# Loading the first group of gates in six parts, ordering one cast behind the U tiles, and multiplying the last V tiles half by half

## The chip, the cores and the metric

The kernel runs on one core of a Trainium2 chip. TensorE (PE in the rows) multiplies, VectorE (DVE) and ScalarE (ACT) do the elementwise work, GpSimd (POOL) issues the indirect gathers, and SyncE (SP) issues every other transfer. PEld is TensorE's weight load. The metric is device time in microseconds (us), the median of several executions; the profile is one further execution with the hardware profiler on. About 0.5% of the time (8 us) is what a measurement of this kernel can tell from no change.

## What is computed

The reference is one layer of a streaming encoder for 544 tokens (512 of a prompt, 32 of a running stream) and 1024 channels. It projects, convolves, attends and normalises, and then applies a "PEER" block, in which this change lies. For each token, 8 heads pick 16 out of 16384 experts each. With `e` the picked rows and `g` the softmax of their scores:

```
a = jnp.einsum('td,thkd->thk', tb, u_tab[e])
a = jax.nn.gelu(a, approximate=False) * g
return jnp.einsum('thk,thkd->td', a, v_tab[e])
```

Then `x = layer_norm(alpha * x + g2 * out)` is stored. `u_tab` and `v_tab` have 16384 rows of 1024 floats, 64 MB each.

## The kernel before, in words

The first 384 tokens (NA, three row tiles, TA = 3) are done densely: every expert is computed for every token, and a gate that is zero where an expert was not picked does the choosing. The other 160 tokens are done by gathers: POOL fetches one expert row per token at a time (`gather`, L893), and DVE multiplies it. The gathers are paced by the dense tiles: each waits for a matmul that an earlier dense tile recorded (ANCHOR).

**Dense work.** The experts are split into 128 tiles j of 128 experts. `u_part(j)` (L953) loads 512 KB of `u_tab`, ACT casts it to a high part `hi` and DVE subtracts to get the low part `lo` (`split`, L943 to L951; three raw buffers, two of hi and lo). PE does 24 matmuls of 384 columns into one of two PSUM tiles `pat` (L959), and ACT evacuates it by Gelu (L965). While 26 tiles have room in SBUF, later results go through one of two buffers `gs` and are stored to `ge_d` in DRAM (L967).

`v_part(j)` (L1012) multiplies that Gelu by the gates (P, DVE, L1025), casts P to Ph (ACT, L1028), subtracts to get Pl (DVE, L1030), and splits 512 KB of `v_tab`. `v_mm` (L1035) then does 18 matmuls of 512 columns for a whole tile: three row tiles i, two halves hf of 512 channels, three products (L1042), each accumulating in one of six PSUM banks `accs[i][hf]` over all j.

**Gates.** `onehots(i)` (L835) makes the gates of 16 tokens at a time: four one-hot tiles on DVE, 32 small matmuls (L874), evacuations into `stg` (L875), and one 1 MB store to `g_d` in DRAM (L876). There are 24 such blocks (NBLK), eight for each row tile i. The gates come back for eight tiles j at a time into a tile `gc` of two buffers (L1013 to L1016): 24 blocks x 128 partitions with 512 bytes each, 1536 KB. The pool of `gc` is opened after the pools of the one-hots are closed (L1002), so that it lies in memory which these used.

**Order.** U tiles run while the one-hots are made, a planner (`slot`, L980) doling out background work between them. When the last gates are made, 8 more U tiles follow (EXTRA, L997); then the V tiles begin, and the U tiles that remain are interleaved with them (L1067 to L1072). The last four V tiles are prepared together (L1084) and multiplied with the row tile i as the outer loop, so that the three row tiles end one after the other. `tail` and `norm_tile` (L1046) then do, for each row tile: a product with g2 for each half (L1050), the sum with x (L1052), the squares on ACT (L1055), and the rest on DVE (L1056 to L1062), then two stores (L1063).

The program is written tile by tile, and a scheduler orders each engine's instructions by a simulated timeline before the program runs. On the chip each engine, and SP's queue of transfers, keeps that order: an instruction that waits holds up all that stand behind it on its engine. A manual dependency of the kind ORD (no semaphore, order alone) can be given to the scheduler. Transfers of SP share one hardware queue (q1), those of POOL another (q0), on the same 16 DMA engines.

Of the kernel before, what the change touches and what calls it, by code (L numbers as in the profile page):

```python
# [13 lines left out]
AF = mybir.ActivationFunctionType  # L14
# [12 lines left out]
NA = 384  # L27
# [14 lines left out]
NBLK = NA // GB  # L42
JC = 8
# [32 lines left out]
def build(tc, I, O):  # L76
# [3 lines left out]
    V, S, G, PE, SY = nc.vector, nc.scalar, nc.gpsimd, nc.tensor, nc.sync  # L80
# [5 lines left out]
    g_d = dram.tile([NBLK, 128, NK, GB], F32, name="g_d")  # L86
# [6 lines left out]
    def pat():  # L93
        return pa.tile([128, 512], F32, tag="pa", name="pat")
# [4 lines left out]
    def sm():  # L99
        return ps.tile([128, 512], F32, tag="sm", name="sm")  # L100
# [136 lines left out]
    U = cp.tile([128, 4, UW], F32, name="U")  # L237
# [28 lines left out]
    ORD = mybir.DependencyInfo(mybir.DependencyClass.NoSync, mybir.DependencyReason.DATA)  # L266
# [45 lines left out]
    for n in range(2):  # L312
        wv = [wsplit(I["w_v"][n, kh]) for kh in range(2)]
        wf = WRAW[-2:]
        for i in range(NT):
            p = pat()
# [7 lines left out]
            else:  # L324
# [6 lines left out]
                p = sm()  # L331
# [249 lines left out]
    for s in range(2):  # L581
        t = op_.tile([128, D], F32, tag="row", name="bg", bufs=4) if s == 0 else xhB[0]
# [356 lines left out]
    h2B = xhB  # L939

    GE = {}

    def split(src, pl=None, nr=RAWB, nh=HIB):  # L943
        pl = pl or uvp
        raw = pl.tile([128, D], F32, tag="raw", name="raw", bufs=nr)
        SY.dma_start(raw, src)
        hi = pl.tile([128, D], F32R, tag="hi", name="hi", bufs=nh)
        S.copy(hi, raw)  # L948
        lo = pl.tile([128, D], F32R, tag="lo", name="lo", bufs=nh)
        V.tensor_sub(lo, raw, hi.bitcast(F32))  # L950
        return hi, lo  # L951

    def u_part(j):  # L953
        hi, lo = split(I["uT"][j])
        p = pat()
        n = 0
        for a, b in ((hi, h2h), (lo, h2h), (hi, h2l)):
            for k in range(KC):
                mm = PE.matmul(p[:, :NA], a[:, k * 128:(k + 1) * 128], b[:, k, :], start=(n == 0), stop=(n == 23))  # L959
                if n == 0:  # L960
                    ANCHOR.append(mm)
                n += 1
        full = sum(g is not None for g in GE.values()) >= ND - 1
        ge = dn.tile([128, NA], F32, tag="gs" if full else "ge", name="ge", bufs=2 if full else ND)
        S.activation(ge, p[:, :NA], AF.Gelu)  # L965
        if full:
            SY.dma_start(ge_d[j], ge)  # L967
            GE[j] = None
        else:
            GE[j] = ge  # L970

# [20 lines left out]
    ahead = 0  # L992
    while state["A"] < TA:
        u_part(ahead)
        ahead += 1
        slot(COST_U, BURST_G)
    for _ in range(EXTRA):  # L997
        u_part(ahead)
        ahead += 1
        slot(COST_U, BURST_G)  # L1000
# [9 lines left out]
    GC = {}  # L1010

    def v_part(j):  # L1012
        if j % JC == 0:  # L1013
            GC[0] = gcp.tile([128, NBLK, JC, GB], F32, tag="gc", name="gc")
            SY.dma_start(GC[0].rearrange("p b j t -> p b (j t)"),
                         g_d[:, :, j:j + JC, :].rearrange("b i j t -> i b (j t)"))  # L1016
        ge = GE.pop(j)
        if ge is None:
            ge = gcp.tile([128, NA], F32, tag="gel", name="gel", bufs=3)
            SY.dma_start(ge, ge_d[j])  # L1020
        early = NK - LAST <= j < NK - 2
        pp, tags = (dn, ("ge",) * 3) if early else (vpp, ("P", "Ph", "Pl"))
        nb = ND if early else 2
        P = pp.tile([128, NA], F32, tag=tags[0], name="P", bufs=nb).rearrange("p (b t) -> p b t", t=GB)
        V.tensor_mul(P, ge.rearrange("p (b t) -> p b t", t=GB), GC[0][:, :, j % JC, :])  # L1025
        Ph = pp.tile([128, NA], F32R, tag=tags[1], name="Ph", bufs=nb)
        Pf = P.rearrange("p b t -> p (b t)")
        S.copy(Ph, Pf)  # L1028
        Pl = pp.tile([128, NA], F32R, tag=tags[2], name="Pl", bufs=nb)
        V.tensor_sub(Pl, Pf, Ph.bitcast(F32))  # L1030
        vp_ = (uvp, RAWB, HIB) if early else (vpp, VRAWB, VHIB)
        vh, vl = split(I["vd"][j * 128:(j + 1) * 128, :], *vp_)
        return Ph, Pl, vh, vl

    def v_mm(j, tiles, parts):  # L1035
        Ph, Pl, vh, vl = parts
        for i in tiles:
            sl = slice(i * 128, (i + 1) * 128)
            for hf in range(2):
                hs = slice(hf * 512, (hf + 1) * 512)  # L1040
                for n, (a, b) in enumerate(((Ph, vh), (Pl, vh), (Ph, vl))):
                    mm = PE.matmul(accs[i][hf], a[:, sl], b[:, hs], start=(j == 0 and n == 0), stop=(j == NK - 1 and n == 2))  # L1042
                    if i == hf == n == 0:
                        ANCHOR.append(mm)
# [21 lines left out]
    for j in range(NK - LAST):  # L1066
        v_mm(j, range(TA), v_part(j))  # L1067
        slot(COST_V)
        while ahead < NK and ahead < j + 3 + lead * (NK - j) // NK:
            u_part(ahead)  # L1070
            ahead += 1
            slot(COST_U)  # L1072
        if ahead == NK and not full:
            full = True
            hx.close()
            fp = pool(ctx, "fp", 1)
            l2g, l2b, g2p, x3, g2s, f3 = [fp.tile([128, D], F32, name=n) for n in ("l2g", "l2b", "g2p", "x3", "g2s", "f3")]
            assert state["gdone"] >= 256
            for dst, src in ((g2p, mod_d[0, 5 * D:6 * D]), (l2g, I["ln2_g"]), (l2b, I["ln2_b"]), (g2s, mod_d[1, 5 * D:6 * D])):
                SY.dma_start(dst, bcast_rows(src, 128))  # L1080
            SY.dma_start(x3, x1_d[TA * 128:TA * 128 + 128])
            norm_tile(3, x3, f3, [accB[0][:, :512], accB[0][:, 512:]], g2p)
    run(gat)
    vs = {j: v_part(j) for j in range(NK - LAST, NK)}  # L1084
    for i in range(TA):
        for j in vs:
            v_mm(j, (i,), vs[j])

    def late(ld):
        tc.add_manual_dep(ld.ins, ANCHOR[-12].ins.name, DEP, reason="paced by the dense tiles")  # L1090
# [13 lines left out]
    for q in range(2):  # L1104
        p = pat()
# [85 lines left out]
```

## Time and profile before

| | us |
|---|---|
| median of 3 runs | 1627.64 (1625.81 to 1632.98) |
| the profiled execution's own time | 1643.86 |
| its span, first to last instruction | 1642.1 |

The profiled execution is 16.2 us (1.0%) longer than the median of the runs. Its span leaves 1.8 us of its own time outside. The rows are of that one execution: they show where time goes and how long each step takes, and a difference worked out from them is taken off the median of the runs.

### The profile page before, as it was taken

The numbers are of one execution on the slowest core, as the hardware profiler recorded it, in microseconds if no ns is written. First come the engines' busy times: TensorE is split into PE (matmuls) and PEld (weight loads), VectorE is DVE, ScalarE is ACT, GpSimd is POOL, SyncE is SP. The second block draws the span as 40 slices with busy tenths as digits, with TensorE's granted clock in tenths as the row PEclk, the third lists the DMA queues.
The fourth block names the chain that finished last, engine by engine and source line by source line (L and its number), as shares of the span: only waits on it lengthen the run. The fifth ranks groups of instructions, "written<-read, shape, count | busy, mean of one in ns | idle before, by whom it ended". The sixth has DMA issues, their size and how long they took to land.

```text
span 1642.1 us, 24695 instructions
## 1 busy us (share of the span) xinstructions
PE 1558.6 (95%) x8887; PEld 1341.7 (82%) x8887; DVE 1387.8 (85%) x2680; ACT 612.7 (37%) x1059; POOL 503.6 (31%) x325
## 2 busy tenths in 40 slices
PE   7999987999989998999899899999999999999996
PEld 4777854786669997999899789888888888888885
DVE  3788888899999997999798568888878787788898
ACT  3312456333122443444445333333333333333342
POOL 0000000000145356259534124544333333344440
PEclk9999987999999999999999999999999999999998
DMA  9767333274478887999999999999999999999993
GB/s 345 281 196 252 89 116 117 87 234 133 153 254 278 289 283 270 329 355 333 332 344 365 372 325 306 344 342 374 332 351 350 338 339 343 341 328 330 347 336 106
DMA packets 184537, 465.58 MB, mean 284 GB/s; under 512 B 17536, under 2 KB 85184, under 8 KB 181216
## 3 DMA queue, kind: packets, MB, share of 16 engines
q1 hardware_dynamic: 138336, 296.23, 52.5%
q0 software_dynamic: 46080, 167.79, 28.9%
q8 instruction: 69, 1.13, 0.3%
q14 instruction: 52, 0.43, 0.1%
HBM read 415.57 MB, written 45.77 MB: 281 GB/s over the span
## 4 chain that ended last, share of the span: by engine, by line
PE 67%; DVE 16%; DMA 7%; issue 6%; ACT 2%; SPq 1%; POOL 0%; DVEq 0%; ACTq 0%; POOLq 0%
PE acc L1042 31%; PE pat L959 22%; PE big L194 3%; PE pat L733 2%; PE big L874 2%; DVE jkg L906 2%; DVE lo L950 2%; DMA rowg<-in_u_ji_dram,idx 1%; PE pat L154 1%; PE big L622 1%; DVE s L712 1%; DVE acc L275 1%; DVE accB L917 1%; DVE IT L714 1%; DMA raw<-in_vd_dram 1%
## 5 line engine op out<-in xcount | busy, mean ns | idle before, releaser
L895 POOL DMA_INDIRECT rowg<-in_u_ji_dram,idx x160 | 205.1, 1282 | 794.1 <-DVE VT L709 441.4
L950 DVE TENSOR_TENSOR lo<-raw,hi 128x1024 fp32r<-128x1024 f32 x256 | 312.9, 1225 | 104.8 <-ACT hi L948 97.8
L895 POOL DMA_INDIRECT rowg<-in_vd_dram,idx x160 | 296.7, 1855 | 297.5 <-DVE accB L917 65.7
L948 ACT CAST hi<-raw 128x1024 fp32r<-128x1024 f32 x256 | 266.8, 1047 | 293.7 <-PE acc L1042 196.8
L1042 PE MATMUL acc<-hi,Pl 128*128 128x512 f32 x768 | 298.1, 391 | 0.0
L1042 PE MATMUL acc<-lo,Ph 128*128 128x512 f32 x768 | 276.3, 389 | 0.0
L1042 PE MATMUL acc<-hi,Ph 128*128 128x512 f32 x768 | 245.6, 391 | 6.6 <-issue 5.2
L959 PE MATMUL pat<-h2h,lo 128*128 128x384 f32 x1024 | 210.6, 343 | 18.7 <-DVE lo L950 18.7
L959 PE MATMUL pat<-h2h,hi 128*128 128x384 f32 x1024 | 210.0, 340 | 4.4 <-ACT ge L965 2.7
L906 DVE SCALAR_TENSOR_TENSOR jkg<-rowg,xhB 128x1024 f16<-128x1024 f32 x160 | 195.3, 1220 | 17.9 <-DMA rowg<-in_u_ji_dram,idx 15.7
L959 PE MATMUL pat<-h2l,hi 128*128 128x384 f32 x1024 | 209.1, 341 | 0.0
L917 DVE SCALAR_TENSOR_TENSOR accB<-rowg,wB,accB 128x1024 f32<-128x1024 f32 x158 | 203.0, 1285 | 6.2 <-DMA rowg<-in_vd_dram,idx 5.7
L959 PEld LDWEIGHTS pat<-h2h,lo 128*128 128x128 f32 x1024 | 182.4, 191 | 22.9 <-DVE lo L950 19.8
L959 PEld LDWEIGHTS pat<-h2h,hi 128*128 128x128 f32 x1024 | 179.3, 188 | 11.6 <-ACT ge L965 3.5
L959 PEld LDWEIGHTS pat<-h2l,hi 128*128 128x128 f32 x1024 | 183.6, 191 | 2.6
L1042 PEld LDWEIGHTS acc<-hi,Ph 128*128 128x128 f32 x768 | 144.3, 189 | 33.1 <-issue 5.5
L1042 PEld LDWEIGHTS acc<-hi,Pl 128*128 128x128 f32 x768 | 145.0, 189 | 27.6 <-issue 0.5
L1042 PEld LDWEIGHTS acc<-lo,Ph 128*128 128x128 f32 x768 | 144.1, 188 | 28.0
L965 ACT ACTIVATE ge<-pat 128x384 f32<-128x384 f32 x128 | 62.7, 491 | 208.9 <-PE pat L959 136.3
L1028 ACT CAST Ph<-P 128x384 fp32r<-128x384 f32 x128 | 65.0, 510 | 145.7 <-issue 81.8
L275 DVE SCALAR_TENSOR_TENSOR acc<-U,wdw,acc 128x574 f32<-128x574 f32 x120 | 96.7, 806 | 1.5
L1030 DVE TENSOR_TENSOR Pl<-P,Ph 128x384 fp32r<-128x384 f32 x128 | 70.8, 554 | 28.3 <-ACT Ph L1028 27.3
(322 smaller groups left out, 1880.3 us busy)
## 6 DMA issues: line engine op xcount, KB each, us to landing
raw<-in_uT_dram SPq DMA_DIRECT2D x128, 512.0 KB
raw<-in_vd_dram SPq DMA_DIRECT2D x128, 512.0 KB
wr<-in_w_ada_dram SPq DMA_DIRECT2D x48, 512.0 KB
g_d<-stg SPq DMA_DIRECT2D x24, 1024.0 KB
gc<-g_d SPq DMA_DIRECT2D x16, 1536.0 KB
wq<-in_w_query_dram SPq DMA_DIRECT2D x32, 512.0 KB
ge_d<-ge SPq DMA_DIRECT2D x70, 192.0 KB
gel<-ge_d SPq DMA_DIRECT2D x70, 192.0 KB
```

The source lines that it names most:

```text
L194: PE.matmul(p[h], a[:, k * 128:(k + 1) * 128], b[:, k, h * HT:(h + 1) * HT], start=(q == 0 and k == 0), stop=(q == 2 and k == KC - 1))
L275: t = V.scalar_tensor_tensor(acc[:, c], U[:, c, w:w + CO], wdw[:, c, w:w + 1], acc[:, c], op0=OP.mult, op1=OP.add)
L895: g = G.indirect_dma_start(out=t, out_offset=None, in_=tab, in_offset=bass.IndirectOffsetOnAxis(ap=idx, axis=0))
L906: V.scalar_tensor_tensor(jk, t, 1.0, h2B[s], op0=OP.mult, op1=OP.mult, accum_out=aB[s][:, q:q + 1])
L917: V.scalar_tensor_tensor(ac, t, w[:, q - c0:q - c0 + 1], ac, op0=OP.mult, op1=OP.add)
L948: S.copy(hi, raw)
L950: V.tensor_sub(lo, raw, hi.bitcast(F32))
L959: mm = PE.matmul(p[:, :NA], a[:, k * 128:(k + 1) * 128], b[:, k, :], start=(n == 0), stop=(n == 23))
L965: S.activation(ge, p[:, :NA], AF.Gelu)
L1028: S.copy(Ph, Pf)
L1030: V.tensor_sub(Pl, Pf, Ph.bitcast(F32))
L1042: mm = PE.matmul(accs[i][hf], a[:, sl], b[:, hs], start=(j == 0 and n == 0), stop=(j == NK - 1 and n == 2))
```

## The change

There are three edits. The first group of gates (j = 0) is loaded by six transfers, of the blocks 0 to 7, 8 to 15, 16 to 19, 20 and 21, 22, and 23, where it was one transfer of all 24; the other 15 groups stay as they are. The cast of the first P to Ph is ordered behind the Gelu of the last U tile issued before the V tiles, which is the eighth extra one. And the last four V tiles are multiplied with the half hf outside the tile j: for each row tile, twelve matmuls of the first half and then twelve of the second, where the halves had alternated with every tile.

```
-        S.activation(ge, p[:, :NA], AF.Gelu)
+        LASTU[0] = S.activation(ge, p[:, :NA], AF.Gelu)
...
-            SY.dma_start(GC[0].rearrange("p b j t -> p b (j t)"),
-                         g_d[:, :, j:j + JC, :].rearrange("b i j t -> i b (j t)"))
+            parts = (0, 8, 16, 20, 22, 23, 24) if j == 0 else (0, NBLK)
+            for b0, b1 in zip(parts, parts[1:]):
+                SY.dma_start(GC[0][:, b0:b1].rearrange("p b j t -> p b (j t)"),
+                             g_d[b0:b1, :, j:j + JC, :].rearrange("b i j t -> i b (j t)"))
...
-        S.copy(Ph, Pf)
+        t = S.copy(Ph, Pf)
+        if j == 0:
+            tc.add_manual_dep(t.ins, LASTU[0].ins.name, ORD, reason="behind the U tiles ahead of V")
...
-    def v_mm(j, tiles, parts):
+    def v_mm(j, tiles, parts, halves=(0, 1)):
...
-            for hf in range(2):
+            for hf in halves:
...
     for i in range(TA):
-        for j in vs:
-            v_mm(j, (i,), vs[j])
+        for hf in range(2):
+            for j in vs:
+                v_mm(j, (i,), vs[j], (hf,))
```

## Rows read from the trace of the kernel before

**Rows 1.** The page's head: span, and each engine's busy time, share and instructions.

```profile
span 1642.1 us, 24695 instructions
PE 1558.6 (95%) x8887; PEld 1341.7 (82%) x8887; DVE 1387.8 (85%) x2680; ACT 612.7 (37%) x1059; POOL 503.6 (31%) x325
```

**Rows 2.** Busy time by stretch around the start of V, then TensorE's granted clock, DMA share, GB/s.

```profile
900.00:930.00 30.00, 25.71 (x151) 25.07 (x148) 16.85 (x15) 9.42 (x13) 8.31 (x8) 1.00 1.06 390
930.00:950.00 20.00, 16.32 (x63) 13.23 (x64) 12.68 (x20) 6.98 (x11) 2.38 (x2) 0.83 1.04 338
950.00:1000.00 50.00, 50.00 (x265) 46.91 (x264) 33.04 (x46) 19.33 (x26) 14.74 (x13) 1.00 0.93 318
```

**Rows 3.** The chain of waits, 880 to 950: start us, us, what.

```profile
907.42 10.81 DMA ge_d<-ge
...
918.80 8.61 PE pat L959 x48
```

**Rows 4.** Timeline of PE: start, us, instruction, count, idle before and what ended it.

```profile
899.75 0.64 PE L874 MATMUL big<-Yg,X 128*128 128x128 f16 x8
...
918.80 1.67 PE L959 MATMUL pat<-h2h,hi 128*128 128x384 f32 x8 [1.70 <-ACT ge L965]
...
932.64 0.76 PE L1042 MATMUL acc<-hi,Ph 128*128 128x512 f32 x1 [5.23 <-issue]
933.20 0.63 PE L1042 MATMUL acc<-hi,Pl 128*128 128x512 f32 x1
...
937.47 0.43 PE L1042 MATMUL acc<-hi,Pl 128*128 128x512 f32 x1
...
948.49 1.66 PE L959 MATMUL pat<-h2h,hi 128*128 128x384 f32 x8 [1.04 <-ACT ge L965]
```

**Rows 5.** Timeline of ACT and DVE around the first P.

```profile
929.01 1.03 DVE L1025 TENSOR_TENSOR P<-ge,gc 128x384 f32<-128x384 f32 x2 [3.42 <-DMA gc<-g_d]
...
929.65 0.94 ACT L1028 CAST Ph<-P 128x384 fp32r<-128x384 f32 x2 [5.32 <-DVE P L1025]
...
931.50 1.04 ACT L948 CAST hi<-raw 128x1024 fp32r<-128x1024 f32 x1 [0.91 <-DMA raw<-in_vd_dram]
...
932.81 1.04 ACT L948 CAST hi<-raw 128x1024 fp32r<-128x1024 f32 x1 [0.27 <-DMA raw<-in_vd_dram]
```

**Rows 6.** Timeline of SP's queue: start of issue, time to issue, transfer.

```profile
901.04 0.32 SPq L876 DMA_DIRECT2D g_d<-stg  x1
...
907.42 3.18 SPq L967 DMA_DIRECT2D ge_d<-ge  x2
...
911.64 0.45 SPq L1015 DMA_DIRECT2D gc<-g_d  x1
912.14 11.37 SPq L946 DMA_DIRECT2D raw<-in_vd_dram  x3
923.55 0.85 SPq L1015 DMA_DIRECT2D gc<-g_d  x1
924.45 12.24 SPq L1020 DMA_DIRECT2D gel<-ge_d  x3
...
937.27 0.38 SPq L967 DMA_DIRECT2D ge_d<-ge  x1
```

**Rows 7.** The page's transfer issues: the gate groups, their number and size.

```profile
gc<-g_d SPq DMA_DIRECT2D x16, 1536.0 KB
```

**Rows 8.** Timeline of PE at its end.

```profile
1629.05 0.39 PE L1042 MATMUL acc<-hi,Pl 128*128 128x512 f32 x1
1629.28 0.39 PE L1042 MATMUL acc<-lo,Ph 128*128 128x512 f32 x1
```

**Rows 9.** Timeline of DVE in the tail.

```profile
1620.64 1.29 DVE L1050 TENSOR_TENSOR ff<-acc,g2p 128x512 f32<-128x512 f32 x2 [0.93 <-PE acc L1042]
...
1623.58 1.37 DVE L1050 TENSOR_TENSOR ff<-acc,g2p 128x512 f32<-128x512 f32 x2 [0.20 <-PE acc L1042]
...
1637.41 1.42 DVE L1062 SCALAR_TENSOR_TENSOR x<-x,st,l2b 128x512 f32<-128x512 f32 x2
```

More of the change, by code (lines that the diff above doesn't have):

```diff
@@ L941, in build @@
     GE = {}
+    LASTU = [None]
     def split(src, pl=None, nr=RAWB, nh=HIB):
```

## The prediction, made before the changed kernel was run

> **What bounds the kernel now.** I read the page's head first: PE is busy for 1558.6 of 1642.1 us [rows 1], so only its idle time and its slow stretches can be won. The views by stretch came next. From 950 to 1000 us PE is busy for 50.00 of 50.00 us, with U and V tiles mixed; around the start of V it is not: 25.71 of 30.00 us from 900 to 930, and 16.32 of 20.00 from 930 to 950, there with a granted clock of 0.83. The DMA share beside it is 1.06 and 1.04 [rows 2]: the transfers are as full as PE is meant to be.
>
> The timeline of PE gives the places [rows 4]. PE idles 1.70 us before the U tile at 918.80, 5.23 us before the first V matmul at 932.64, and 1.04 us before 948.49. After the long idle the matmuls run slowly: from 933.20 to 937.47 there are ten steps of 0.427 us, where steps at the full clock take 0.23 us (1629.05 to 1629.28) [rows 4, 8]. That is the lower of the clock's two levels, 1.2 against 2.4 GHz. Ten steps of 0.20 us and a first one of 0.56 for 0.23 lost 2.33 us.
>
> The chain of waits and the other timelines say why. The U tile at 918.80 waited for a Gelu, which waited for a store of an earlier result (issued 907.42, 10.81 us on its way) to free one of two buffers [rows 3, 4]. V waited for the gates: the group was issued at 911.64, and the first P had it at 929.01, 17.4 us later; Ph followed at 929.65 [rows 5, 6]. The `v_tab` load issued right behind, at 912.14, let its cast start at 931.50 [rows 5, 6]. So SP's transfers come one after the other through a full queue: what stands ahead delays what stands behind.
>
> The tail is the other place. DVE idles 0.93 and 0.20 us before the products of the first two row tiles and has little idle after that; PE's last matmul starts at 1629.28 and DVE's last pair at 1637.41 [rows 8, 9].
>
> **The change, part by part.** The durations are of the profiled execution (1643.86 us, of which 1642.1 are its span); the runs' median is 16.2 us less, and I take the sum off that median.
>
> *Six parts.* All but the last part need only gates stored before 901.04, the last store [rows 6]. Their memory was the one-hots', which the last one-hot matmul at 899.75 frees [rows 4]. So 23 of 24 blocks can enter the queue some 10 us earlier, and the last, 64 KB, stands where the whole load stood, with the same wait for the last store; behind that wait on SP are the three `v_tab` loads, the second group and the loads of spilled results, as before [rows 6]. Five more issues cost SP at most 0.85 us each, the longest issue of a group [rows 6], 4.25 us; they are hidden by the queue itself, which held SP for 11.37 and 12.24 us at the next issues. Without that cover they would delay the stores of U results by as much.
>
> What is gained: V no longer waits for the gates. With all of the two later holes gone, 5.23 + 2.33 + 1.04 = 8.60 us.
>
> What is paid: the early parts stand ahead of `u_tab` loads and of the store issued at 907.42. A group is 1536 KB, 1.573 MB [rows 7]; 23/24 of it at the stretch's 390 GB/s [rows 2] takes 3.86 us. The price is between 0 (they fill gaps in the queue) and 23/24 of the store's 10.81 us, 10.4 us. I take 3.86, as the share of 1.06 leaves no gaps. The 1.70 us hole becomes 5.56 us. A hole of 5.23 us brought the slow clock and one of 1.70 did not [rows 4]; 5.56 is nearer to the former, so 2.33 us more are paid (between 0 and 2.33).
>
> The Trainium skill has a rule against this edit (DMA: Bandwidth & Descriptors, Bandwidth): batch transfers to at least 1 MiB, since 64 KB reach only 138 GB/s. It also gives about 2.0 us of fixed time for each transfer (Anatomy of one DMA), so that by an estimate from that page five more would take 10 us if nothing overlapped. The two queued `v_tab` loads of this case disagree, 1.31 us apart.
>
> In rows: those casts, at 931.50 and 932.81 [rows 5], both waited for their loads, and 524 KB in 1.31 us is 400 GB/s, about the stretch's mean. A queued transfer below 1 MB pays nothing visible here. I take 0; the other end is a rival below.
>
> *The order of the cast.* Ph(0) now stands behind the eighth extra Gelu on ACT. From 900.2 to 927.4 PE does six U tiles in 27.2 us (two took 8.61 [rows 3]): two that the loop began, and four of the eight. Four more, 4 x 4.17 = 16.7 us, move ahead of V. The edit adds no instruction. What is queued behind the cast waits with it: on ACT the next Ph and the casts of `v_tab`, on DVE Pl(0), on PE all V tiles. POOL's gathers are paced by whichever dense tiles run, so they go on through the U tiles. Moved U tiles cost nothing as long as their loads, and the stores of their results, keep pace. The step from the last Gelu to Ph and V costs between 0 and 1.04 us (the idle before 948.49, where PE also waited for a Gelu [rows 4]); I take 0, since the mixed stretch after 950 has no idle [rows 2] and a later U tile can fill it.
>
> *Half by half.* The 72 matmuls, their weight loads and operands stay. The first half of each row tile is complete 12 matmuls earlier, 2.7 us, so DVE can do its product while PE does the second. DVE is then nearly full to its end, so what can go is its waiting, 0.93 + 0.20 = 1.13 us [rows 9]; below, 0, or a loss of that size if the fourth tile's operands, now wanted at the tenth matmul instead of the nineteenth, come late. I take 0.93, the longer wait. SP's final stores move with DVE.
>
> *Sum.* -8.60 + 3.86 + 2.33 - 0.93 = -3.34 us, so 1627.64 - 3.34 = 1624.3 us. A measurement here can tell about 0.5%, 8.1 us, from no change: the forecast is **no measurable difference**.
>
> **The rivals.**
>
> *A: the holes simply close.* The early parts cost nothing, and the clock never falls: -8.60 - 0.93 = -9.5 us, 1618.1; with the 1.70 us hole and all of the tail's waits gone, -11.4 and 1616.2. For it: four more U tiles give PE 16.7 us of work just where it had none. Against: the DMA share of 1.06.
>
> *B: V is held back behind starved U tiles, slower.* The fifth extra U tile needs a PSUM buffer, hence the Gelu of the third, hence room in `gs`, hence the store of the first. That store was issued at 937.27, behind the second gate group (923.55) and three loads that held SP for 12.24 us [rows 6]. If that order stays, PE finishes the fourth tile at 927.4 + 3.9 = 931.3 and then has nothing, as V may not start. It goes on between 941 (an early landing, 3.7 us after the issue) and 948.5, where it went on before [rows 4]; four tiles later, at 957.7 to 965.2, V starts after 1.0 us of casts. Before, the same work was behind PE at 932.64 + 16.7 + 2.33 + 1.04 = 952.7. So V comes 6.0 to 13.5 us late; less the tail's 0.93, 1632.7 to 1640.2. It decides where that store stands in SP's order: ahead of the second group, no loss. For it: SP's order before. Against: the scheduler works out a new order.
>
> *C: the parts come no earlier.* SP's order may leave them at 911.64, or their memory may come free late. Then the split does nothing, the order alone moves U tiles into the holes or gives as much back, and the time is 1627.64 - 0.93 = 1626.7.
>
> *D: each part occupies the queue for a fixed time.* With 1.31 us for each of five more, as for a 512 KB load, 6.6 us join the delay: 1624.3 + 6.6 = 1630.9. The page's fixed time of about 2.0 us is of this kind; its rule is named above.
>
> **How the numbers follow.** Forecast 0.35, A 0.28, B 0.20, C 0.12, D 0.05. A is faster by over 0.5% (below 1619.5); B is counted as slower, though its near end is not over 0.5% (above 1635.8); the rest is within. So faster 0.28, same 0.52, slower 0.20. The range reaches down past A's end of 1616.2 by the runs' own scatter (1.8 us), to 1614, and up to the middle of B, 1637, and leaves out the upper half of B and what no case holds. The likeliest case's own range: with its price at 0, 1620.4; at 10.4 us, 1630.8.
>
> **What would show it.** The split is right if five parts are issued between 900 and 905 and the first P no longer waits for a gate group. The price is right if PE's idle before the third extra U tile grows from 1.70 us to about 5.6. The order is right if eight U tiles follow the last one-hot's two before any V matmul, and the 5.23 us hole with its slow steps is gone. B is right if PE idles for about 10 us or more before the fifth of these tiles, with a store of `ge_d` as the cause. The half order is right if DVE's first product of each row tile starts before PE has ended that tile. I am wrong if the idle between 900 and 970 falls below 2 us, or if stretches after 970, where PE is full, get holes that no edit touches.

## The result, and the profile after

The changed kernel is **slower**: 1643.15 us median of 6 runs (1637.81 to 1644.88), against 1633.43 of the kernel before in 6 runs beside it; ratio 1.0067, interval 1.0046 to 1.0087. That is 7.5 to 14.2 us. The forecast was 1624.3, no measurable difference; the time lies above the range's upper end of 1637. Of the 18.9 us between the two, 5.8 are the base: the forecast was taken off a median of 1627.64 from three runs, and before's median beside the change is 1633.43. Rival B, V held back behind starved U tiles, had 0.20.

The two profiled executions can't be set against each other as wholes: 1643.86 us for before, 1642.47 for after. The order of each engine's instructions is the same in both programs up to SP's first load of gates, yet before's execution reached the last one-hot matmul at 899.75 [rows 4] and after's at 880.95. Before's had lost time in two holes that after's does not have (e2's and e4's below have one such each); why only some executions have them is not shown. Timeline of PE, before:

```profile
650.59 2.93 PE L959 MATMUL pat<-h2h,lo 128*128 128x384 f32 x8 [6.80 <-DVE lo L950]
...
802.77 2.93 PE L959 MATMUL pat<-h2h,lo 128*128 128x384 f32 x8 [5.73 <-DVE lo L950]
```

So I compare from the last one-hot matmul on. The head of the page and the busy time by stretch of the changed kernel (after the engines: granted clock, DMA share, GB/s) answer to [rows 1, 2]:

```profile
span 1639.7 us, 24733 instructions
...
PE 1552.5 (95%) x8887; PEld 1335.9 (81%) x8887; DVE 1386.2 (85%) x2680; ACT 611.5 (37%) x1059; POOL 474.3 (29%) x325
```

```profile
900.00:930.00 30.00, 13.12 (x65) 12.80 (x66) 12.52 (x16) 5.32 (x7) 4.27 (x5) 0.72 1.09 366
930.00:950.00 20.00, 18.01 (x103) 17.37 (x101) 11.04 (x16) 6.65 (x10) 4.28 (x4) 1.00 0.76 246
950.00:1000.00 50.00, 50.00 (x243) 43.91 (x242) 38.29 (x50) 16.18 (x23) 17.98 (x16) 1.00 0.89 302
```

PE is busy for 13.12 of 30.00 us where before it was for 25.71 [rows 2], while the DMA share is still above 1. From 950 to 1000 both are full. The timeline of PE shows one long hole, in answer to [rows 4]:

```profile
880.95 0.63 PE L874 MATMUL big<-Yg,X 128*128 128x128 f16 x8
...
899.83 1.66 PE L960 MATMUL pat<-h2h,hi 128*128 128x384 f32 x8 [1.52 <-ACT ge L966]
...
925.31 2.93 PE L960 MATMUL pat<-h2h,hi 128*128 128x384 f32 x8 [16.88 <-ACT ge L966]
928.03 2.08 PE L960 MATMUL pat<-h2h,lo 128*128 128x384 f32 x8
929.95 1.55 PE L960 MATMUL pat<-h2l,hi 128*128 128x384 f32 x8
931.33 1.55 PE L960 MATMUL pat<-h2h,hi 128*128 128x384 f32 x8
...
937.18 1.66 PE L960 MATMUL pat<-h2h,hi 128*128 128x384 f32 x8 [1.53 <-ACT ge L966]
...
946.24 1.67 PE L960 MATMUL pat<-h2h,hi 128*128 128x384 f32 x8 [0.46 <-ACT ge L966]
```

The tile at 925.31 is the fifth extra U tile. Idle times sum to 1.52 + 16.88 + 1.53 + 0.46 = 20.39 us. After the long one, two groups of eight matmuls take 2.72 and 1.92 us, step to step, where the next eight take 1.38: 1.88 us more. The granted clock of the first of these stretches is 0.50, the lower level, and 1.00 in the last (views by stretch):

```profile
925.31:928.03 2.72, 2.72 (x8) 2.72 (x9) 2.65 (x5) 0.49 (x1) 1.16 (x1) 0.50 1.04 416
929.95:931.33 1.38, 1.38 (x9) 1.38 (x9) 0.00 (x0) 0.00 (x0) 0.00 (x0) 1.00 1.05 406
```

With the idle times that is 22.27 us. The same sum for before is 1.70 + 5.23 + 1.04 + 2.33 = 10.30 [rows 4, 8]. The difference, 11.97 us, lies within the measured 7.5 to 14.2. It is not all that sets these two executions apart: from the last one-hot matmul to the end they take 742.3 and 758.8 us. The changed kernel's has two more holes, at 1005.14 (0.63 us) and here, with some 2 us of slow steps behind it:

```profile
1048.00 1.16 PE L1047 MATMUL acc<-hi,Ph 128*128 128x512 f32 x3 [1.80 <-ACT Ph L1031]
```

Before's has one of 1.41 us at 1590.83. These later holes are not the slowdown's cause: e1 below has the same loss without the two. SP's queue and ACT say where it comes from; SP's rows answer to [rows 6]:

```profile
892.79 10.66 SPq L1018 DMA_DIRECT2D gc<-g_d  x6
903.49 1.52 SPq L947 DMA_DIRECT2D raw<-in_vd_dram  x3
907.06 0.38 SPq L1018 DMA_DIRECT2D gc<-g_d  x1
908.73 8.02 SPq L1023 DMA_DIRECT2D gel<-ge_d  x2
916.84 0.38 SPq L947 DMA_DIRECT2D raw<-in_uT_dram  x1
917.26 0.43 SPq L1023 DMA_DIRECT2D gel<-ge_d  x1
917.79 0.38 SPq L968 DMA_DIRECT2D ge_d<-ge  x1
```

```profile
922.66 1.04 ACT L949 CAST hi<-raw 128x1024 fp32r<-128x1024 f32 x1 [8.18 <-DMA raw<-in_uT_dram]
924.76 0.49 ACT L966 ACTIVATE ge<-pat 128x384 f32<-128x384 f32 x1 [1.06 <-DMA ge_d<-ge]
```

The Gelu that frees PE's PSUM buffer runs at 924.76. It waited for the store issued at 917.79, and ahead of it on ACT stood a cast that waited 8.18 us for weights issued at 916.84. Both issues stand behind all that V loads first: gates, `v_tab` tiles, the second group, stored Gelus. Before the change PE did V in this stretch and did not wait for that queue, with no idle time from 932.64 to 947.45; now V may not start.

### The profile page after: what moved, and what is told of

Read it like the earlier page. It is cut to its first block, busy times and chain, and to the rows that moved or that the text cites. A ratio compares the mean times of both kernels' runs of the same rounds, so it can differ in the third digit from the quotient of the medians.

```text
span 1639.7 us, 24733 instructions
## 1 busy us (share of the span) xinstructions
PE 1552.5 (95%) x8887; PEld 1335.9 (81%) x8887; DVE 1386.2 (85%) x2680; ACT 611.5 (37%) x1059; POOL 474.3 (29%) x325
## 4 chain that ended last, share of the span: by engine, by line
PE 66%; DVE 13%; DMA 10%; issue 5%; ACT 3%; SPq 1%; POOL 1%; DVEq 0%; ACTq 0%; POOLq 0%
PE acc L1047 27%; PE pat L960 23%; PE big L194 3%; PE pat L733 2%; PE big L874 2%; DMA raw<-in_vd_dram 2%; DMA rowg<-in_u_ji_dram,idx 2%; PE pat L194 2%; DVE jkg L906 1%; DVE lo L951 1%; DMA raw<-in_uT_dram 1%; PE pat L154 1%; DVE s L712 1%; PE big L622 1%; DVE accB L917 1%
## 5 line engine op out<-in xcount | busy, mean ns | idle before, releaser
L895 POOL DMA_INDIRECT rowg<-in_u_ji_dram,idx x160 | 214.4, 1340 | 777.8 <-DVE VT L709 436.2
L895 POOL DMA_INDIRECT rowg<-in_vd_dram,idx x160 | 258.1, 1613 | 323.1 <-PE acc L1047 97.4
L1047 PE MATMUL acc<-lo,Ph 128*128 128x512 f32 x768 | 290.9, 390 | 0.0
L1047 PE MATMUL acc<-hi,Ph 128*128 128x512 f32 x768 | 238.8, 390 | 1.8 <-ACT Ph L1031 1.8
L917 DVE SCALAR_TENSOR_TENSOR accB<-rowg,wB,accB 128x1024 f32<-128x1024 f32 x158 | 202.1, 1279 | 17.9 <-DMA rowg<-in_vd_dram,idx 17.5
L960 PE MATMUL pat<-h2l,hi 128*128 128x384 f32 x1024 | 204.6, 339 | 0.0
L1035 DVE TENSOR_TENSOR Pl<-P,Ph 128x384 fp32r<-128x384 f32 x128 | 70.6, 552 | 19.4 <-ACT Ph L1031 17.4
```

Of the source, the lines that this page charges most:

```text
L895: g = G.indirect_dma_start(out=t, out_offset=None, in_=tab, in_offset=bass.IndirectOffsetOnAxis(ap=idx, axis=0))
L917: V.scalar_tensor_tensor(ac, t, w[:, q - c0:q - c0 + 1], ac, op0=OP.mult, op1=OP.add)
```

## The experiments

Each kernel was timed in 5 rounds beside the kernel before on the same chip. "Hole" is the longest idle time of PE between the last one-hot matmul and the mixed stretch, "sum" all of its idle times over 0.3 us there, "end" the time from the start of PE's last row in its timeline (the last V matmul; in e6 and e7 the four matmuls of the sample tile) to the end of the span, all of the one profiled execution. Holes behind that stretch, 0 to 6.7 us in all, are in none of these columns.

| kernel | hole | sum | end | median | ratio (interval) |
|---|---|---|---|---|---|
| before | 5.23 | 7.97 | 12.8 | - | 1 |
| changed | 16.88 | 20.39 | 13.2 | 1643.15 | 1.0067 (1.0046 to 1.0087) |
| e1 order alone | 17.69 | 21.78 | 12.9 | 1643.13 | 1.0064 (1.0043 to 1.0086) |
| e2 parts alone | 5.30 | 7.85 | 13.0 | 1636.00 | 1.0023 (1.0000 to 1.0045) |
| e3 halves alone | 5.45 | 8.00 | 12.8 | 1636.21 | 1.0024 (0.9997 to 1.0052) |
| e4 changed, V's later loads behind the stores | 10.27 | 13.37 | 13.2 | 1635.84 | 1.0014 (0.9992 to 1.0036) |
| e5 changed, four `gs` | 14.06 | 15.57 | 13.2 | 1638.15 | 1.0053 (1.0029 to 1.0077) |
| e6 before, four `gs` | 1.67 | 3.18 | 24.2 | 1633.93 | 1.0025 (1.0003 to 1.0047) |
| e7 before, V's later loads behind the stores | 5.65 | 7.17 | 24.2 | 1642.57 | 1.0075 (1.0049 to 1.0102) |
| e8 order alone, four `gs` | 14.65 | 16.16 | 12.9 | 1635.32 | 1.0028 (1.0009 to 1.0046) |
| e9 as e6, sample rows ahead | 1.51 | 2.03 | 17.3 | 1633.05 | 0.9976 (0.9951 to 1.0001) |
| e10 order alone, V's loads from GpSimd | 10.63 | 17.39 | 12.9 | 1642.49 | 1.0032 (1.0005 to 1.0058) |
| e11 as e8, U's weights ahead | 3.73 | 5.24 | 17.5 | 1631.03 | 0.9988 (0.9968 to 1.0009) |
| e12 as e9, sample rows further ahead | 1.65 | 3.16 | 14.6 | 1624.53 | 0.9945 (0.9923 to 0.9968) |

The medians belong to different chips: before's were 1632.88 beside e1 to e4, 1631.63 beside e5 to e8, 1638.87 beside e9 and e10, and 1632.19 beside e11 and e12. The ratios are what compares.

### Which of the three parts costs

e1 keeps the changed kernel's order of the cast and undoes the rest; e2 and e3 keep the parts and the halves alone. On the changed kernel, e1 and e3 undo the parts:

```diff
-            parts = (0, 8, 16, 20, 22, 23, 24) if j == 0 else (0, NBLK)
+            parts = (0, NBLK)
```

e2 and e3 undo the order of the cast:

```diff
-        if j == 0:
-            tc.add_manual_dep(t.ins, LASTU[0].ins.name, ORD, reason="behind the U tiles ahead of V")
```

e1 and e2 undo the halves:

```diff
-        for hf in range(2):
-            for j in vs:
-                v_mm(j, (i,), vs[j], (hf,))
+        for j in vs:
+            v_mm(j, (i,), vs[j])
```

> Theory (the order): with V held behind the last Gelu, PE has nothing between the fourth and the fifth extra U tile, because the fifth needs a PSUM buffer that a Gelu frees only when the first extra tile's store has landed, and that store stands behind the second gate group on SP. The idle before the fifth extra tile is 10 to 17 us, as in the changed kernel (16.88 us), and the time is 8 to 12 us above the kernel before (ratio 1.005 to 1.007). Rival (the parts): six transfers in place of one hold up SP's queue, so that the order alone, with one load, is within 2 us of the kernel before and has no idle over 6 us there.

> Theory (the order): the parts stand where the one load stood in SP's order, so that V starts at about the same place: idle of 4 to 7 us before the first V matmul, as before (5.23 us), and a time within 2 us of the kernel before. Rival (the parts): the six parts take some 10 us to issue, the first P or the stores come late by as much, and the time is 8 to 12 us above (ratio 1.005 to 1.007).

> Both theories: the stretch around the start of V is as before. For the tail: if the waits of DVE for a row tile's second half were on the path, 0.9 us are won; if the tail is a full row of DVE work, the time from PE's last matmul to the end stays at 12.8 to 13.2 us and the time is within 1 us of the kernel before. I expect the latter.

The order alone gives a loss as large, 1.0064 against 1.0067, and the same hole (17.69 us, 0.7 over the range I gave), in the timelines of PE and of SP:

```profile
928.61 2.93 PE L960 MATMUL pat<-h2h,hi 128*128 128x384 f32 x8 [17.69 <-ACT ge L966]
```

```profile
894.95 0.38 SPq L1018 DMA_DIRECT2D gc<-g_d  x1
895.38 11.34 SPq L947 DMA_DIRECT2D raw<-in_vd_dram  x3
906.77 0.43 SPq L1018 DMA_DIRECT2D gc<-g_d  x1
907.24 12.66 SPq L1023 DMA_DIRECT2D gel<-ge_d  x3
...
920.48 0.38 SPq L968 DMA_DIRECT2D ge_d<-ge  x1
```

The parts win nothing. V's first matmul still waits 5.30 us in e2 and 5.45 in e3, which loads the gates whole. From the first gate load's issue to the first P it is 17.68 us with six parts in e2 (915.24 - 897.56; timelines of SP and of DVE):

```profile
897.56 11.01 SPq L1018 DMA_DIRECT2D gc<-g_d  x6
```

```profile
915.24 1.03 DVE L1028 TENSOR_TENSOR P<-ge,gc 128x384 f32<-128x384 f32 x2 [3.86 <-DMA gc<-g_d]
```

and 17.4 with one load [rows 5, 6]. Nor do they hold up what stands behind them: from that issue to the first extra tile's store is 25.00 us with six parts (917.79 - 892.79 in the changed kernel) and 25.53 with one in e1 (920.48 - 894.95). The time that SP stood at `v_tab`, 11.34 us, it now stands at the parts, 10.66.

The halves win nothing either: the end stays 12.8 us long. DVE's timeline in e3 shows waits of 0.94 and 0.41 us at the products, where before had 0.93 and 0.20 [rows 9]:

```profile
1606.73 1.89 DVE L1053 TENSOR_TENSOR ff<-acc,g2p 128x512 f32<-128x512 f32 x3 [0.94 <-PE acc L1045]
...
1610.36 0.69 DVE L1053 TENSOR_TENSOR ff<-acc,g2p 128x512 f32<-128x512 f32 x1 [0.41 <-PE acc L1045]
```

Both ratios are a little over 1, 3 to 4 us, where I had expected to be within 2 and 1 us; with intervals that reach 1.0000 and below, neither can be told from no change.

### Is it the store, and its place in SP's queue

e4 orders the second gate group and the first six loads of stored Gelus behind the last extra tile's store; e7 does that to the kernel before. In e4:

```diff
-            SY.dma_start(ge_d[j], ge)
+            LASTST[0] = SY.dma_start(ge_d[j], ge)
...
+    AHEAD = [LASTST[0].ins.name]
...
-                SY.dma_start(GC[0][:, b0:b1].rearrange("p b j t -> p b (j t)"),
-                             g_d[b0:b1, :, j:j + JC, :].rearrange("b i j t -> i b (j t)"))
+                ld = SY.dma_start(GC[0][:, b0:b1].rearrange("p b j t -> p b (j t)"),
+                                  g_d[b0:b1, :, j:j + JC, :].rearrange("b i j t -> i b (j t)"))
+                if j == JC:
+                    tc.add_manual_dep(ld.ins, AHEAD[0], ORD, reason="behind the stores of the U tiles ahead")
...
-            SY.dma_start(ge, ge_d[j])
+            ld = SY.dma_start(ge, ge_d[j])
+            if j < ND + 6:
+                tc.add_manual_dep(ld.ins, AHEAD[0], ORD, reason="behind the stores of the U tiles ahead")
```

e5 (changed kernel), e6 (before) and e8 (order alone) give `gs` four buffers instead of two, so that a Gelu waits for a store two tiles further back:

```diff
-        ge = dn.tile([128, NA], F32, tag="gs" if full else "ge", name="ge", bufs=2 if full else ND)
+        ge = dn.tile([128, NA], F32, tag="gs" if full else "ge", name="ge", bufs=4 if full else ND)
```

> The changed kernel with the second gate group and the first six loads of spilled results ordered on SP behind the store of the last U tile ahead of V. Theory (the order, through the stores): the idle of 16.88 us before the fifth extra U tile falls below 4 us, V starts after all eight with no wait for its gates, and the time is 4 to 8 us below the kernel before (ratio 0.995 to 0.998), 14 to 18 us below the changed one. Rival (the parts, or the full queue itself): the stores still land late, the idle only moves to another U tile, and the time stays 6 us or more above the kernel before.

> The kernel before (one load, no order of the cast, halves alternating) with the second gate group and the first six loads of spilled results behind the store of the last U tile ahead of V on SP. Theory (V held back costs, not these loads): with V free to start when its gates land, the late group is not what costs here; idle of 5 to 7 us before the first V matmul stays, and the time is within 3 us of the kernel before. Rival (the second group and the loads are what stands in the way): the stores land sooner, the idle around V's start falls by 4 us or more and the ratio is 0.997 or less.

> The changed kernel with four buffers for results that are stored (gs) in place of two. Theory (the order's price is paid through the two buffers): a Gelu no longer waits for the store of two tiles earlier, the fifth extra U tile starts without the idle of 16.88 us (below 4 us), and the time falls by 10 us or more against the changed kernel, to the kernel before or below it (ratio 0.994 to 1.001). Rival (SP's full queue itself, whatever the buffers): U tiles wait for their own loads behind the gates, idle of 8 us or more stays there, and the ratio stays at 1.004 or above.

> The kernel before with four buffers gs in place of two, and nothing of the change. Theory (the buffers): the idle of 1.70 and 1.04 us where PE waits for a Gelu goes; the idle before the first V matmul (5.23 us) falls below 2 us, as further U tiles can run while V waits for its gates: 5 to 10 us won (ratio 0.994 to 0.997). Rival (the gates alone set V's start): the 5 us before the first V matmul stay, and the time is within 2 us of the kernel before.

> The order of the cast alone (one load, halves alternating), with four buffers gs. Theory: with buffers the order costs little: no idle above 4 us before any of the extra U tiles, time at or below the kernel before (ratio 0.994 to 1.001), where the order with two buffers had 1.0064. Rival (holding V back costs by itself): ratio 1.004 or above, as with two buffers.

None of these five runs met its theory's numbers in full: the hole stayed in e4, e5 and e8, and e6 and e7, with holes as expected, missed on the time. e5 came out as its rival said (1.0053).

e4 supports the chain nonetheless. The store comes 17.15 us after the first gate part instead of 25.00, 7.9 us sooner; the hole is 6.6 us shorter, and the ratio falls from 1.0067 to 1.0014, 8.7 us. It does not close to the 4 us expected, as the gates themselves and `v_tab` still stand ahead, on SP and, with the casts of `v_tab`, on ACT. Timelines of SP, PE and ACT:

```profile
898.33 12.59 SPq L1020 DMA_DIRECT2D gc<-g_d  x6
910.96 1.62 SPq L948 DMA_DIRECT2D raw<-in_vd_dram  x3
...
915.48 0.33 SPq L969 DMA_DIRECT2D ge_d<-ge  x1
```

```profile
924.28 2.93 PE L961 MATMUL pat<-h2h,hi 128*128 128x384 f32 x8 [10.27 <-ACT ge L967]
```

```profile
918.99 1.04 ACT L950 CAST hi<-raw 128x1024 fp32r<-128x1024 f32 x1 [8.05 <-DMA raw<-in_vd_dram]
```

Four buffers take the store out of the chain, and the hole hardly shrinks: in e5 and e8 another wait takes its place. Timelines of PE, ACT and SP in e8:

```profile
936.13 2.93 PE L960 MATMUL pat<-h2h,hi 128*128 128x384 f32 x8 [14.65 <-ACT hi L949]
```

```profile
935.03 1.04 ACT L949 CAST hi<-raw 128x1024 fp32r<-128x1024 f32 x1 [12.09 <-DMA raw<-in_uT_dram]
```

```profile
914.31 0.55 SPq L1018 DMA_DIRECT2D gc<-g_d  x1
914.97 11.46 SPq L968 DMA_DIRECT2D ge_d<-ge  x1
926.48 1.39 SPq L1023 DMA_DIRECT2D gel<-ge_d  x3
927.96 0.85 SPq L947 DMA_DIRECT2D raw<-in_uT_dram  x2
```

This hole is three tiles later than e1's, and it waits for the eighth extra tile's weights, issued at 927.96. So my theory of the store was too narrow: whatever a U tile needs stands behind V's first loads. In e6, with four buffers and no order, the scheduler lets seven of the eight extra tiles run ahead of V and only the eighth behind it; PE idles 3.18 us in all. Under four buffers the order thus adds 13.0 us of idle time (16.16 against 3.18), and under two 13.8 (21.78 against 7.97).

Yet e6 did not become faster, and e7 is slower. The end says why: 24.2 us in both, against 12.8. The program's order had moved the sample tile's matmuls (`accB` times `selrep`) from the middle of the last V tiles to behind them. PE in e7:

```profile
1616.51 0.40 PE L1051 MATMUL acc<-lo,Ph 128*128 128x512 f32 x1
1616.75 1.88 PE L1115 MATMUL pat<-accB,selrep 128*128 128x512 f32 x4
```

The normalisation of that tile then follows PE's last matmul. In e7 that is 11.4 us more, against 12.2 measured (1.0075). So e7 tells nothing against the chain: its hole is before's, 5.65.

### Is it the issue order or the bytes

e10 takes e1 and issues the first two gate groups and the first stored Gelus from GpSimd's queue:

```diff
-                SY.dma_start(GC[0][:, b0:b1].rearrange("p b j t -> p b (j t)"),
+                (G if j <= JC else SY).dma_start(GC[0][:, b0:b1].rearrange("p b j t -> p b (j t)"),
...
-            SY.dma_start(ge, ge_d[j])
+            (G if j < ND + 6 else SY).dma_start(ge, ge_d[j])
```

e11 takes e8, and orders V's first loads on SP behind the weights of the eighth extra tile (and the sample tile's matmuls as in e9, below):

```diff
-        SY.dma_start(raw, src)
+        LASTLD[0] = SY.dma_start(raw, src)
...
+    AHEAD = LASTLD[0].ins.name
+
+    def behind(ld):
+        tc.add_manual_dep(ld.ins, AHEAD, ORD, reason="behind the weights of the U tiles ahead")
...
+                if j <= JC:
+                    behind(ld)
...
+            if j < ND + 6:
+                behind(ld)
...
+        if j < 4:
+            behind(LASTLD[0])
```

> The order of the cast alone, as in e1, but the first two gate groups and the first six loads of a stored Gelu are issued from GpSimd's queue instead of SP's; same bytes, same order on PE up to a tile's half. Theory (SP's queue: the store of a Gelu and the next uT load stand behind the gates and those loads, which hold SP 11 to 12 us each): the hole of 17.69 us before the starved U tile falls under 7 us, and the time from 1643.1 to 1632 to 1637. Rival (the 16 DMA engines are full there, share 1.09 in the changed kernel, so that the bytes come no sooner whoever issues them): the hole stays over 12 us and the time over 1639.

> The order of the cast with four buffers gs, as in e8, and on SP's queue V's first loads (two gate groups, the first stored Gelus, the first tiles of vd) ordered behind the weights of the eighth extra U tile; the sample tile's four matmuls written ahead of the last V tiles, as in e9. In e8 PE stood 14.65 us for the weights of a U tile that SP issued only at 927.96, behind the gates and three stored Gelus. Theory (what a U tile needs stands behind V's loads on SP): that hole falls under 4 us, none over 4 us opens before V, and the time is 1622 to 1629. Rival (the same bytes have to be in before V may start, whatever their order): the hole only moves to V's start, the idle time between the last one-hot matmul and V stays over 10 us, and the time is 1632 or more.

e10 lies between theory and rival. The hole falls to 10.63 us (under 7 and over 12 were expected), but a second one of 4.31 opens, and the sum falls only from 21.78 to 17.39. The ratio is 1.0032 where e1's is 1.0064, with intervals that overlap; its median is over the rival's 1639, but before's beside it was high too (1638.87). Timelines of SP, POOL and ACT:

```profile
892.03 1.38 SPq L947 DMA_DIRECT2D raw<-in_vd_dram  x3
```

```profile
892.77 2.94 POOL L1018 DMA_DIRECT2D gc<-g_d  x2 [2.52 <-issue]
```

```profile
907.59 1.99 ACT L949 CAST hi<-raw 128x1024 fp32r<-128x1024 f32 x2 [5.89 <-DMA raw<-in_vd_dram]
...
918.18 0.49 ACT L966 ACTIVATE ge<-pat 128x384 f32<-128x384 f32 x1 [0.51 <-DMA ge_d<-ge]
```

SP hardly stands at an issue any more, but the `v_tab` loads issued at 892.03 let ACT go on only at 907.59, with two groups of gates, 3.1 MB, in flight beside them; ACT's next casts and the Gelu at 918.18 come late behind that. So the issue is part of the wait and the bytes are part of it; how it divides is not settled by this run.

e11's holes are those of the first theory. The eighth tile has no hole at all, its weights being issued at 913.88, ahead of the gates, and V waits 3.73 us. Timelines of PE and SP:

```profile
933.29 2.27 PE L1059 MATMUL acc<-hi,Ph 128*128 128x512 f32 x6 [3.73 <-issue]
```

```profile
913.88 0.33 SPq L948 DMA_DIRECT2D raw<-in_uT_dram  x1
914.32 0.55 SPq L1024 DMA_DIRECT2D gc<-g_d  x1
```

The idle time did not move to V: it went from 16.16 us in e8 to 5.24, under the rival's 10. All eight tiles are ahead of V as the change wants, and the same bytes are loaded. The ratio fell from 1.0028 to 0.9988, with intervals that just touch. Later losses offset some of the gain: an end 4.6 us longer than e8's, and later holes of 6.7 us in all against 2.9. The median of 1631.03 is 2 us over the range I gave.

### A version that beats both

e9 and e12 are before with four buffers and the sample tile's matmuls written ahead of the last V tiles. In e9 the lines are moved, and nothing else:

```diff
+    ab = accB[1]
+    pss = []
+    for q in range(2):
+        p = pat()
+        PE.matmul(p, selrep, ab[:, q * 512:(q + 1) * 512], start=True, stop=True)
+        pss.append(p)
     for i in range(TA):
         for j in vs:
             v_mm(j, (i,), vs[j])
```

In e12 every matmul of the last two row tiles is ordered behind them (`sel` is the last of them):

```diff
-            v_mm(j, (i,), vs[j])
+            v_mm(j, (i,), vs[j], sel if i >= TA - 2 else None)
...
+                    if behind is not None:
+                        tc.add_manual_dep(mm.ins, behind.ins.name, ORD, reason="behind the rows of the sample tile")
```

> Before with four buffers gs, and the four one-row matmuls of the sample tile (accB times selrep) written ahead of the last four V tiles instead of behind them; neither the order of the cast nor the parts nor the halves. Theory: four buffers alone (1633.93 us) took three more U tiles ahead of V, lost only 1.51 + 1.67 us there, and gave the gain back at the end, because these matmuls stood behind V's last: 24.2 us from PE's last matmul to the end against 12.8 in before. With 29 matmuls of V behind them again the end should be 13 to 18 us long and the time 1622 to 1628, 0.2 to 0.6 per cent under before. Rival: the end isn't where the gain went; then the end gets shorter and PE ends later by as much, and the time stays at 1631 to 1636.

> As e9 (before with four buffers gs), with the sample tile's matmuls ordered ahead of all matmuls of the last two row tiles, so that 48 of V's matmuls stand behind them instead of 29. In e9 the end was 17.3 us long; DVE finished accB at 1593.9 and then idled 3.92 us. Theory: the sample tile's rows move into that idle time, the end takes 14 to 16 us, and the time is 1 to 3 us under e9, 0.3 to 0.5 per cent under before. Rival: accB is late by then, PE waits for it, and nothing is won or up to 2 us lost against e9.

Both ends came out as expected, 17.3 and 14.6 us, and the ratios followed: 1.0025 (e6), 0.9976, 0.9945 as the end went from 24.2 to 17.3 to 14.6. e9's median of 1633.05 is over the range I gave, but so was before's beside it; its ratio is within. Its interval still touches 1; that of e12 does not. PE, and DVE's wait in front of the products, in e12:

```profile
1596.29 1.88 PE L1091 MATMUL pat<-accB,selrep 128*128 128x512 f32 x4
...
1608.70 0.39 PE L1042 MATMUL acc<-lo,Ph 128*128 128x512 f32 x1
```

```profile
1596.25 1.29 DVE L1052 TENSOR_TENSOR ff<-acc,g2p 128x512 f32<-128x512 f32 x2 [0.55 <-PE acc L1042]
```

DVE's wait there was 3.92 us in e9; it is 0.55 here. e12 is 1624.53 us against before's 1632.19 beside it, 0.55 per cent less, a little more than I had expected. It has none of the change's three parts: with a sum of 3.16 us against before's 7.97 it wins at V's start what the order was meant to win, by letting a U tile's store come later rather than by holding V back.

## Why the prediction was wrong

**Six parts: the first step failed.** I wrote that 23 of 24 blocks "can enter the queue some 10 us earlier", as their memory comes free with the last one-hot matmul. They may have been able to; they did not. The first part is issued 11.84 us after the start of that matmul (892.79 - 880.95), the whole load before 11.89 us (911.64 - 899.75 [rows 4, 6]). All six stand in SP's order where the one load stood. The gain of 8.60 us did not come for that reason, and the price of 3.86 us was not paid either: the hole before the third extra tile is 1.52 us, where it was 1.70. The premise of rival C was right; its time was not, as C let the order cost nothing. That the parts' issues cost nothing held: 25.00 us against 25.53 to the store.

**Rival D, and the page behind it.** The Trainium skill gives a transfer a fixed time of about 2.0 us (DMA: Bandwidth & Descriptors, Anatomy of one DMA, for the path that GpSimd issues; these are SP's), so that by an estimate from that page five more would have taken 10 us unless they overlapped. The traces show no such time in a full queue: 25.00 us to the store with six parts, 25.53 with one. My own 0 held, and D's 1.31 us for each part did not come.

**The order of the cast: this is the step that decided.** I wrote that moved U tiles cost nothing "as long as their loads, and the stores of their results, keep pace", took it that they do, and put the term at 0. They don't: the hole before the fifth extra tile is 16.88 us, and with the order alone (e1) it is 17.69. Rival B had named that tile, the store and the loads ahead of it, with an idle time of 9.7 to 17.2 us and V 6.0 to 13.5 us late; measured, V's stretch lost 11.97 us more. B's near end had the store landing 3.7 us after its issue, for which it showed no row; the Gelu that needed it started 7.0 us after the issue (924.76 - 917.79). Against B I had set that the scheduler works out a new order. It left SP's order there as [rows 6] show it, and that row deserved more than 0.20. What B lacked is that the weights of the next tiles stand behind the same loads (e8): its cure, the store ahead of the second group "no loss", left a hole of 10.27 us in e4.

**The step from Gelu to Ph** cost PE nothing: Ph follows at 946.57, right behind the Gelus at 945.70, and a ninth U tile keeps PE busy until V, as I had said a later tile can. The 0.46 us stand before that tile, which waited for a Gelu, and that for a store.

**Half by half.** The 0.93 us were not won; e3 shows the same wait at the first product, 0.94. The end is 12.8 us long with either order, as the work of DVE and ACT behind PE's last matmul sets it: DVE's last product starts 1.6 us behind that matmul's start in both (1630.89 and 1616.94), held by the row tile before and not by PE.

**The clock.** I took the slow steps with the hole. That held: after 16.88 us of idle time PE ran at the lower level (0.50), and its matmuls took 1.88 us more than the same ones after them. But a hole's length alone does not tell: slow steps followed the 1.80 us at 1048.00 (granted clock 0.58 from there to 1052.00), and none the 1.70 before 918.80 [rows 4].

**My sign of being wrong.** I had named holes after 970 that no edit touches. The changed kernel's execution has them, 0.63 and 1.80 us; e1's has neither and is as slow, so the sign came true without being the cause.

## What to carry to other kernels

Before an engine's work is reordered to fill a hole, read in the queue of transfers what the moved work itself will need, inputs and the stores that free its buffers both, and what stands ahead of it there: V's stretch was a cover for a full queue, and the U tiles put in its place starved behind V's own loads. An order that is right on one engine needs its loads ordered to match; in e11 it then had no cost that the runs can tell (0.9988), and no gain over e9, which goes without it (0.9976). And where a scheduler fills in the rest, look at the far end too: a change at 900 us moved four matmuls at 1600 us and made the end 11 us longer.

## What the runs showed that I had not expected

Giving V's first loads to GpSimd's queue took only 4.4 us off PE's idle time of 21.8 (e10): the first of three 512 KB loads, issued by an SP that hardly waited, reached its cast some 15 us later (892.03 to 907.59) while 3.1 MB of gates were on their way. And two edits far from the end, four buffers and the order of some loads, each lengthened the end of the kernel before from 12.8 to 24.2 us (e6, e7); together with the order of the cast neither did (e4, e5, e8).
